# A fixed order for TensorE in the second pass's heads, and a head's output matmuls one step later

## The chip, the cores and the metric

The kernel runs on one core of one Trainium2 chip. The metric is the device time of one execution in microseconds; lower is better. The figure given for a kernel is the median of several runs, and one further execution is recorded by the hardware profiler. Every line of a profile that is shown here comes from that recorded execution.

## The reference

One layer of a decoder trunk, for one sequence of 2048 tokens and a width of 1024, all in fp32. Cut to what matters:

```python
h = rms_norm(x, g_pre) * (1.0 + scale) + shift
pv, pg, hq, hf, hi, hg, mg_pool, mg_hgrn = split(h @ w_in)      # 1024 -> 7168

# branch A: pooling over windows of 2, 4, 8, 16, gated by silu(pg)
branch_a = (multiscale_pool(pv) @ pool_w * pool_scale * silu(pg)) @ w_pool_o

# branch B: 8 heads of 128, gated linear recurrence
f = lb + (1 - lb) * sigmoid(hf);  k = 1 - f;  q = silu(hq);  v = hi
S_t = diag(f_t) S_{t-1} + k_t v_t^T;   o_t = S_t^T q_t
branch_b = (rms_norm(o, hgrn_norm_g) * silu(hg)) @ w_hgrn_o

y = (sigmoid(mg_pool) * branch_a + sigmoid(mg_hgrn) * branch_b) @ w_out
x = x + gate * rms_norm(y, g_post)
```

The recurrence is evaluated in chunks. Within a chunk the output is (decayed scores of q and k) times v, and between chunks a 128 x 128 state per head is decayed and added to.

## The kernel before, in words

**Passes and stages.** The 2048 tokens are worked in two passes of 1024 (`p` = 0, 1), and each pass in two halves of 512 (`t` = 0, 1; `T` = 512). A pass projects V for all heads, then runs eight heads one after the other, then the projection of branch B and the output projection y. In the profiled execution the heads of the first pass run from 124 to 742 us, what follows of that pass (and V of the second) to 978, the heads of the second pass to 1582, and its projections to the end.

**Weight products.** A weight product is 12 matmuls of 128x512: four blocks of the contraction, three matmuls each, since the activations and weights are held as a high and a low part (`three`). `quad` makes a 2 x 2 block product of the weights and activations out of seven such products (a Strassen scheme) in three PSUM banks: `pa` (B11), `pe` (T1), `pa` (T2), `pb` (B21), `pa` (T3), `pe` (B22), `pa` (T4). Between them ScalarE copies a bank to SBUF (`c22`, `c12`, and `pb` from `pa`), and VectorE adds. A head has three quads: `fq` (gates f and q), `m` (the merge gates) and `gp` (the head's output gate, and pooling), in this order; head 7 has `fq`, `gp`, `m`. A name ends in pass, head and half, so `pam1_3` is the bank `pa` of quad `m` in pass 1 (the second), head 3; the listings of the order below drop the pass and keep the head and the half.

**The recurrence beside the products.** `hgrn(p, h, t, cx)` is a generator that holds one head's recurrence for one half. It is advanced to its next `yield` by each call of `tick()`, and `quad` ticks once after most of its products, so the small matmuls of a head lie between the products of that head and of the next. Both halves go side by side. In the order of a head:

- four steps of scores (`psa`, five ticks apart): in each, 16 matmuls for each half that use 32 columns of TensorE's array; VectorE puts them under a mask into `PT`, and prepares the next operands `X`;
- transposes of K (`pk`), the state's increments (`pd`, 4 matmuls for each half), and VectorE's chain of states (`SC`);
- two ticks later the output matmuls (`po`, 8 for each half), ScalarE's squares with their sums (`junk`, `ss`) and a power on GpSimd;
- two ticks later ScalarE's scaled copies (`on`); two ticks later their transposes (`pot`), VectorE's gate product (`sgg<-pot`) and SyncE's store of the gated half.

A head's last steps fall into the `m` and `gp` quads of the head behind it, beside that head's first scores.

**What sets the order.** The source gives the program's order, and the tile framework's scheduler sets the order on each engine when the kernel is built: an instruction may be issued ahead of one that stands before it in the program. `after(ins)` is a context in which every new instruction is ordered behind `ins`:

```python
    def after(ins):
        return tc.issue_after(ins.ins) if ins is not None else nullcontext()
```

It is an edge for the scheduler; on one engine it puts no wait into the program. Before the change it is used around V's products, the adaLN products and a few others, not in the heads. All matmuls of products and of the recurrence go through `mm`, so they carry its line in the profile (L345; the transposes are L810 for `pk` and L846 for `pot`). PSUM has eight banks: four for the products (`pj`), two for `psa` (`ph`) and two shared by `pk`, `pd`, `po` and `pot` (`px`).

Of the kernel before, what the change touches and what calls it, by code (L numbers as in the profile page):

```python
# [18 lines left out]
P = 128  # L19
# [52 lines left out]
def tile_block(ctx: ExitStack, tc: tile.TileContext, x, c, w_ada, b_ada, g_pre, g_post, w_in,  # L72
# [3 lines left out]
    V, A, G, PE, SP = nc.vector, nc.scalar, nc.gpsimd, nc.tensor, nc.sync  # L76
# [16 lines left out]
    def utile(name, dt=F32):  # L93
        return up.tile([P, T], dt, tag="u", name=name)
# [4 lines left out]
    def after(ins):  # L99
        return tc.issue_after(ins.ins) if ins is not None else nullcontext()  # L100
# [23 lines left out]
    ident = cst.tile([P, P], F32, name="ident")  # L124
# [138 lines left out]
    def factor_step(steps):  # L263
        flush_due()
        once(steps)
# [67 lines left out]
    def take(look=LOOK):  # L333
# [7 lines left out]
        ready[i] = None  # L341
        return w if isinstance(w, tuple) else (w[:, 0:T], w[:, T:2 * T])

    def mm(o, l, r, start, stop):
        return PE.matmul(o, lhsT=l, rhs=r, start=start, stop=stop, skip_group_check=True)  # L345

    def three(ps, w, rhs, start, stop):

# [38 lines left out]
    def ada_mul(q):  # L387

        for kk in range(KT):
            o = psa[1][32 * (kk % 4):32 * (kk % 4) + 32, :]  # L390
            it = PE.matmul(o, lhsT=cz[:, kk, :], rhs=parts[q][kk], start=kk < 4, stop=kk >= 4, skip_group_check=True)
        sums[q] = utile(f"ar{q}")
        behind["ar"] = A.copy(sums[q], psa[1])
        return it

    def ada_done(q):
        r = sums.pop(q)
        for j in range(4):
            it = PE.transpose(psa[0][:, j * P:(j + 1) * P], r[:, j * P:(j + 1) * P], ident)
        v = small[:, 56:60]  # L400
        V.tensor_reduce(v, psa[0].rearrange("p (j a b) -> p j a b", j=4, b=32)[:, :, :, 0], axis=AX.X, op=ADD)
        sl = slice(q * 2, q * 2 + 2)
        V.tensor_tensor(shv[:, sl], v[:, 0:2], col("bsh")[:, sl], op=ADD)
        V.tensor_tensor(scv[:, sl], v[:, 2:4], col("bsc")[:, sl], op=ADD)
        iv = V.scalar_tensor_tensor(scv[:, sl], scv[:, sl], 1.0, col("gpre")[:, sl], op0=ADD, op1=MUL)
        return it, iv
# [6 lines left out]
    def pv_load(g):  # L413
        wt = [utile(f"pvt{g}_{z}") for z in range(2)]
        for z in range(2):
            SP.dma_start(wt[z], w_pv_t[g * P:(g + 1) * P, z * T:(z + 1) * T])
        return wt
# [75 lines left out]
    def xsq(tok, xs):  # L493

        s2 = sp.tile([P, 2], F32, tag="xss", name=f"xss{tok}")
        for n in range(2):
            jx = sp.tile([P, T], BF16, tag="jx", name=f"jx{tok}_{n}", bufs=1)
            A.activation(jx, xs[n], AF.Square, scale=1.0 / 32, accum_out=s2[:, n:n + 1])
        r = rst[:, tok:tok + 1]
        G.tensor_scalar(r, s2[:, 0:1], s2[:, 1:2], EPS, op0=ADD, op1=ADD)  # L500
        tt(r, r, mh[:, 0:1], op=ALU.pow, e=G)
        return r

    def x_rows(tok, load):
        xs = [utile(f"x{tok}_{n}") for n in range(2)]
        for n in range(2):
            load(xs[n], x[tok * P:(tok + 1) * P, n * T:(n + 1) * T])
        return xs
# [52 lines left out]
    def x_stats(tok):  # L561
        xsq(tok, x_rows(tok, gated))
# [105 lines left out]
    def hgrn(p, h, t, cx):  # L668
# [6 lines left out]
        K = utile("K" + n)  # L675
# [5 lines left out]
        o = 0  # L681
# [112 lines left out]
        for cc in range(NT):  # L794
            o = cc * P
# [11 lines left out]
        yield  # L807
        pk = px.tile([P, T], F32, tag="px", name="pk" + n)
        for cc in range(NT):
            PE.transpose(pk[:, cc * P:(cc + 1) * P], K[:, cc * P:(cc + 1) * P], ident)  # L810
        KS = utile("KS" + n)
        A.copy(KS, pk)
        yield
# [6 lines left out]
        for cc in range(NT):  # L820
            nxt = SC[:, cc * P:(cc + 1) * P]
            V.scalar_tensor_tensor(nxt, sts[-1], Tb[128][:, cc:cc + 1], pd[:, cc, :], op0=MUL, op1=ADD)
            sts.append(nxt)
        yield
        yield
        po = px.tile([P, NT, P], F32, tag="px", name="po" + n)
# [12 lines left out]
        on = utile("on" + n)  # L839
# [3 lines left out]
        yield  # L843
        pot = px.tile([P, T], F32, tag="px", name="pot" + n)
        for cc in range(NT):
            PE.transpose(pot[:, cc * P:(cc + 1) * P], on[:, cc * P:(cc + 1) * P], ident)  # L846
        og = cx["G"].pop((h, t))
        V.scalar_tensor_tensor(og, pot, col("ng"), og, op0=MUL, op1=MUL)
        two_out("G", p, h, t, og, cx, h == NH - 1)
# [3 lines left out]
    def pv_got(p, g, t, u, cx):  # L853
        n = f"{p}_{g}_{t}"
        w = WINDOWS[g]
        PV = qp.tile([P, HALO + T], F32, tag="qr", name="PV" + n)
        A.copy(PV[:, 0:HALO], halo[:, g, :])
        A.copy(PV[:, HALO:], u)
        A.copy(halo[:, g, :], PV[:, T:T + HALO])
        cur, lo = PV, 0  # L860
        sh = 1
        while sh < w:
            nx = qp.tile([P, HALO + T], F32, tag="qr", name=f"W{sh}_{n}")
            lo += sh
            tt(nx[:, lo:], cur[:, lo:], cur[:, lo - sh:HALO + T - sh], op=ADD)
            cur = nx
            sh *= 2
        pm = utile("pm" + n)
        V.scalar_tensor_tensor(pm, cur[:, HALO:], 1.0 / w, PV[:, HALO:], op0=MUL, op1=SUB)
        if p == 0 and t == 0:  # L870
            e0 = pm[:, 0:HALO]
            tt(e0, cur[:, HALO:2 * HALO], icnt[:, g * HALO:(g + 1) * HALO])
            tt(e0, e0, PV[:, HALO:2 * HALO], op=SUB)
        cx["pw"][g, t] = pm

    def pg_got(p, g, t, u, cx):
        n = f"{p}_{g}_{t}"
        sg = utile("spg" + n)
        A.activation(sg, u, AF.Sigmoid)
        tt(sg, u, sg)  # L880
        V.scalar_tensor_tensor(sg, cx["pw"].pop((g, t)), col("psc", g), sg, op0=MUL, op1=MUL)
        two_out("P", p, g, t, sg, cx, g == NG - 1)

    def g_got(p, h, t, u, cx):
        sg = utile(f"sgg{p}_{h}_{t}")
        A.activation(sg, u, AF.Sigmoid)
        tt(sg, u, sg)
        cx["G"][h, t] = sg
# [42 lines left out]
    def v_head(p, h, cx):  # L931
        vt = vp.tile([P, 8, P], F32, tag="v", name=f"V{p}_{h}")
        gated(vt, cx["Vd"][:, :, h * P:(h + 1) * P], "Vd")
        cx["V"][h] = vt
# [91 lines left out]
    def two_split(nm, i, cx):  # L1026
        for t in range(2):
            hi, lo = cx["g" + nm][i, t]
            split(lo.bitcast(F32), hi, lo)
# [261 lines left out]
    def once(steps):  # L1291

        if steps:
            steps.pop(0)()
# [10 lines left out]
    it = ada_mul(0)  # L1305
    with after(ix), after(ic):
        prep()
    with after(it), after(ix):
        it, iv = ada_done(0)
# [45 lines left out]
    for p in range(NPASS):  # L1355
# [60 lines left out]
        def htick():  # L1416
            tick()
            every[0] += 1
            if every[0] % 11 in (1, 3, 5, 7, 9):
                factor_step(behind_heads)  # L1420

        for h in range(NH):
            if 0 < h < NH - 1:
                v_head(p, h + 1, cx)
            n = f"{p}_{h}"

            def fq(row, t, u):
                (f_got, q_got)[row](p, h, t, u, cx)

            def gp(row, t, u):  # L1430
                if row == 1:
                    g_got(p, h, t, u, cx)
                elif h % 2 == 1:
                    pg_got(p, h // 2, t, u, cx)
                else:
                    pv_got(p, h // 2, t, u, cx)

            wt = pv_load(h // 2) if p == 0 and h % 2 == 0 else None
            steps = []

            def tick_in():
                htick()
                once(steps)

            quad("fq" + n, cx, fq, htick)
            if h == 0:
                for z in range(2):
                    v_head(p, z, cx)
            active.extend(hgrn(p, h, t, cx) for t in range(2))
            if wt:  # L1450
                pv_merge(h // 2, wt)
            htick()
            for i, kind in enumerate(KINDS[h == NH - 1]):
                if kind == "gp":
                    quad("gp" + n, cx, gp, htick)
                else:
                    if h == NH - 1:
                        steps += [lambda: None]
                        steps += [lambda g=g: two_in("P", p, g, cx) for g in range(NG - 1)]
                        steps += [lambda g=g: two_split("P", g, cx) for g in range(NG - 1)]  # L1460
                    quad("m" + n, cx, lambda row, t, u: m_got(p, h, row, t, u, cx), tick_in)
                htick()
            while steps:
                once(steps)
            if p + 1 < NPASS:
                x_stats(8 + h)
        for j in range(KT):
            if j > 0:
                two_in("G", p, j - 1, cx)
            if j > 1:  # L1470
                g_half(p, j - 2, cx)
                if j % 2 == 1:
                    forms("g", j // 2 - 1, cx["g32"])
            a_job(p, j, cx)
            factor_step(behind_heads)
# [101 lines left out]
```

## Time and profile before

| | before |
|---|---|
| median of 3 runs | 1743.84 us (1743.43 to 1744.43) |
| profiled execution | 1744.35 us |
| its span | 1742.6 us |
| mean granted TensorE clock | 0.999 |
| TensorE matmuls, busy | 1714.9 us (98% of the span) |
| TensorE weight loads, busy | 1402.0 us (80%) |
| VectorE busy | 1220.8 us (70%) |
| ScalarE busy | 852.3 us (49%) |
| GpSimd busy | 101.5 us (6%) |
| HBM | 243 GB/s over the span |

The span runs from the first to the last instruction of the recorded execution, and the time of that execution adds what lies around it. An engine's busy time is the time in which it has an instruction under way; matmuls are pipelined, and their ends are modelled, so 98% does not say that TensorE runs at its peak. Matmul records are counted in passes through the array: an fp32 matmul of scores or state shows as two records.

### The profile page before, as it was taken

Reading aid. Unit: us, or ns where it says so; the run is one execution under the profiler, and the core shown is the slowest. Engines: PE = TensorE matmul, PEld = TensorE weight load, DVE = VectorE, ACT = ScalarE, POOL = GpSimd, SP = SyncE. Lnnn points to the kernel's source line nnn. Section 1 sums busy time; section 2 is a strip of 40 time slices with the busy share of each in tenths; the row PEclk is TensorE's granted clock in tenths of the full one; section 3 lists DMA queues with packets and bytes.
Section 4 is the critical chain, followed back from the end, with each engine's and each line's share of the span. In section 5 each row is a group of like instructions: output and inputs, shape, how many; then the busy total and the mean of one; then the engine's idle time right before and its main releaser. Section 6 shows DMA issues by size and latency. Waiting matters only on the chain.

```text
span 1742.6 us, 31732 instructions
## 1 busy us (share of the span) xinstructions
PE 1714.9 (98%) x11805; PEld 1402.0 (80%) x11805; DVE 1220.8 (70%) x2546; ACT 852.3 (49%) x1975; POOL 101.5 (6%) x152
## 2 busy tenths in 40 slices
PE   7999999999999999999999999999999999999998
PEld 4788888888887887877887888888788888888886
DVE  4668898897988889778787255455455545676666
ACT  4756656566565665343755325344243353434243
POOL 1100001000100100100030000000000000000002
PEclk9999999999999999999999999999999999999999
DMA  9759787788779787976895765665665655575657
GB/s 311 269 177 327 282 322 266 292 298 312 267 285 337 261 286 283 341 263 209 277 309 169 250 203 181 202 199 169 218 194 170 215 174 195 176 236 164 215 193 266
DMA packets 191288, 425.33 MB, mean 244 GB/s; under 512 B 19311, under 2 KB 44572, under 8 KB 191134
## 3 DMA queue, kind: packets, MB, share of 16 engines
q1 hardware_dynamic: 181918, 406.52, 68.3%
q10 hardware_dynamic: 9216, 16.78, 2.6%
q8 instruction: 93, 1.52, 0.4%
q14 instruction: 61, 0.50, 0.1%
HBM read 267.51 MB, written 155.71 MB: 243 GB/s over the span
## 4 chain that ended last, share of the span: by engine, by line
PE 88%; DMA 5%; DVE 4%; ACT 1%; issue 1%; SPq 0%; POOL 0%; DVEq 0%; POOLq 0%; ACTq 0%
PE pafq L345 10%; PE pam L345 9%; PE pagp L345 9%; PE pefq L345 5%; PE pem L345 5%; PE pegp L345 5%; PE psA L345 4%; PE ray L345 4%; PE psa L345 3%; PE psV L345 3%; PE raB L345 3%; PE po L345 3%; PE pbfq L345 3%; PE pbm L345 2%; PE pbgp L345 2%; PE raV L345 2%
## 5 line engine op out<-in xcount | busy, mean ns | idle before, releaser
L181 DVE TENSOR_TENSOR whl<-wr,whl 128x512 fp32r<-128x512 f32 x160 | 109.0, 688 | 47.4 <-ACT whl L181 45.8
L345 PE MATMUL pagp<-hT,whl 128*128 128x512 f32 x384 | 128.2, 395 | 1.1 <-DVE c22gp L490 0.8
L345 PE MATMUL pam<-hT,whl 128*128 128x512 f32 x384 | 129.0, 397 | 0.1
L181 ACT CAST whl<-wr 128x512 fp32r<-128x512 f32 x160 | 99.1, 622 | 59.2 <-issue 15.3
L345 PE MATMUL pafq<-hT,whl 128*128 128x512 f32 x384 | 126.3, 390 | 0.0
L724 DVE COPY_PREDICATED PT<-mask,psa 128x256 f32<-128x256 uint8 x160 | 86.0, 546 | 46.4 <-PE psa L345 46.4
L181 ACT CAST whl<-wri 128x512 fp32r<-128x512 f32 x76 | 47.2, 623 | 119.3 <-PE psA L345 28.0
L345 PEld LDWEIGHTS pagp<-hT,whl 128*128 128x128 f32 x384 | 72.1, 188 | 17.2 <-issue 1.2
L345 PEld LDWEIGHTS pam<-hT,whl 128*128 128x128 f32 x384 | 72.2, 188 | 15.0 <-ACT c12m L626 0.3
L345 PEld LDWEIGHTS pafq<-hT,whl 128*128 128x128 f32 x384 | 72.1, 188 | 15.1
L345 PE MATMUL psA<-Ph,whl 128*128 128x512 f32 x256 | 82.3, 395 | 0.6 <-ACT Ph L181 0.4
L345 PE MATMUL psV<-whl,hB 128*128 128x512 f32 x256 | 79.6, 394 | 1.2 <-ACT hB L1315 1.1
L490 DVE TENSOR_TENSOR K<-K,TT 128x256 f32<-128x256 f32 x192 | 80.2, 422 | 0.4 <-PE psa L345 0.4
L345 PE MATMUL pagp<-lT,whl 128*128 128x512 f32 x192 | 74.9, 390 | 0.0
L345 PE MATMUL pam<-lT,whl 128*128 128x512 f32 x192 | 74.9, 390 | 0.0
L345 PE MATMUL pafq<-lT,whl 128*128 128x512 f32 x192 | 74.7, 389 | 0.0
L345 PEld LDWEIGHTS psa<-X,K 128*32 128x32 f32 x2816 | 50.0, 110 | 26.5 <-issue 20.2
L181 DVE TENSOR_TENSOR whl<-wri,whl 128x512 fp32r<-128x512 f32 x76 | 51.6, 683 | 26.0 <-ACT whl L181 25.2
L835 POOL TENSOR_SCALAR ss<-ss 128x4 f32<-128x4 f32 x32 | 14.3, 448 | 878.2 <-ACT junk L834 878.0
L672 DVE TENSOR_SCALAR F<-F 128x512 f32<-128x512 f32 x16 | 6.8, 426 | 78.1 <-ACT F L671 78.0
L345 PE MATMUL psa<-X,K 128*32 128x48 f32 (+2 forms) x2816 | 60.6, 208 | 0.5 <-DVE PT L718 0.5
L345 PEld LDWEIGHTS psV<-whl,hB 128*128 128x128 f32 x256 | 47.5, 188 | 13.9 <-issue 1.7
(569 smaller groups left out, 4810.3 us busy)
## 6 DMA issues: line engine op xcount, KB each, us to landing
wr<-in_w_quad_dram SPq DMA_DIRECT2D x88, 256.0 KB, 5.0
whl<-scr_y SPq DMA_DIRECT2D x36, 512.0 KB, 4.6
sm<-Sd SPq DMA_DIRECT2D x64, 256.0 KB, 5.4
whl<-scr_b SPq DMA_DIRECT2D x32, 512.0 KB, 3.3
scr_y<-rfy SPq DMA_DIRECT2D x40, 256.0 KB, 3.0
x<-in_x_dram SPq DMA_DIRECT2D x32, 256.0 KB, 3.7
wa<-in_w_ada_dram SPq DMA_DIRECT2D x32, 256.0 KB, 6.1
V<-Vd SPq DMA_DIRECT2D x16, 512.0 KB
```

Source lines behind the costliest of these rows:

```text
L181: return A.copy(hi, src32), (e or V).tensor_tensor(lo, src32, hi.bitcast(F32), op=SUB)
L345: return PE.matmul(o, lhsT=l, rhs=r, start=start, stop=stop, skip_group_check=True)
L490: return (e or V).tensor_tensor(o, a, b, op=op)
L672: V.tensor_scalar(F, F, 1e-30, None, op0=MAX)
L724: V.copy_predicated(dst.rearrange("p (c q) a b -> p c q a b", c=NT), m, src.rearrange("p c (a b) -> p c a b", b=b).unsqueeze(2) .broadcast ...
L835: G.tensor_scalar(ss, ss, 1.0 / P, EPS, op0=MUL, op1=ADD)
```

## The change

It has two parts. First, `mm` and a new `turn` (a transpose) put every TensorE instruction of the second pass's heads behind the one that the program issued before it, so there TensorE's order is the program's; `line["on"]` is set ahead of the heads loop when `p > 0` and cleared behind it. Second, `hgrn` has one more `yield` ahead of `po`, in both passes: the output matmuls and all that follows in that head come one tick later.

```diff
+    line = {"on": False, "it": None}
+
     def mm(o, l, r, start, stop):
-        return PE.matmul(o, lhsT=l, rhs=r, start=start, stop=stop, skip_group_check=True)
+        with after(line["it"] if line["on"] else None):
+            line["it"] = PE.matmul(o, lhsT=l, rhs=r, start=start, stop=stop, skip_group_check=True)
+        return line["it"]
+
+    def turn(o, i):
+        with after(line["it"] if line["on"] else None):
+            line["it"] = PE.transpose(o, i, ident)
...
         for cc in range(NT):
-            PE.transpose(pk[:, cc * P:(cc + 1) * P], K[:, cc * P:(cc + 1) * P], ident)
+            turn(pk[:, cc * P:(cc + 1) * P], K[:, cc * P:(cc + 1) * P])
...
             sts.append(nxt)
+        yield
         yield
         yield
         po = px.tile([P, NT, P], F32, tag="px", name="po" + n)
...
         for cc in range(NT):
-            PE.transpose(pot[:, cc * P:(cc + 1) * P], on[:, cc * P:(cc + 1) * P], ident)
+            turn(pot[:, cc * P:(cc + 1) * P], on[:, cc * P:(cc + 1) * P])
...
+        line.update(on=p > 0, it=None)
         for h in range(NH):
...
+        line["on"] = False
         for j in range(KT):
```

Eight lines come in ahead of `three` and one in `hgrn`, so `mm` is L348 after, `turn` L353, `junk` L843 and `on` L850.

**TensorE, second pass, around `pegp` of head 3.** A row is one instruction or a run of alike ones: line, operation, out<-in, tile of the array or of the output, count. `pagp` and `pegp` are products of the quad `gp`, `psa` the scores of head 3 (`psa_0` and `psa_1` are its halves), `pot` the transposes of head 2's output. Before, the first product of `gp` ends and the second stands between the scores:

```order
L345 MATMUL pagp_3_13346<-lB_3_9933,whl_13221 128x512
L345 MATMUL pagp_3_13346<-hB_3_9932,whl_13221 128x512
L345 MATMUL psa_0_10924<-X_1_3_0_13257,K_3_0_13062 32x48 x2
L345 MATMUL pegp_3_13363<-hT_0_10287,whl_13288 128x512
...
L345 MATMUL pegp_3_13363<-hT_3_10378,whl_13288 128x512
L345 MATMUL psa_0_10924<-X_1_3_0_13257,K_3_0_13062 32x48 x14
L345 MATMUL psa_1_10925<-X_1_3_1_13282,K_3_1_13069 32x48 x16
L345 MATMUL pagp_3_13346<-hT_0_10405,whl_13315 128x512
```

After, at the end of `pegp`:

```order
L348 MATMUL pegp_3_13349<-lT_3_10379,whl_13288 128x512
L348 MATMUL pegp_3_13349<-hT_3_10378,whl_13288 128x512
L353 MATMUL pot_2_0_13366<-ident,on_2_0_13322 128x128 x4
L353 MATMUL pot_2_1_13373<-ident,on_2_1_13327 128x128 x4
L348 MATMUL psa_0_10924<-X_1_3_0_13257,K_3_0_13062 32x48 x16
L348 MATMUL psa_1_10925<-X_1_3_1_13282,K_3_1_13069 32x48 x16
L348 MATMUL pagp_3_13332<-hT_0_10405,whl_13305 128x512
```

The scores, in two groups around `pegp` before, are one group behind it, and `pot`, which stood ahead of `pagp`, stands right ahead of them. The same holds around `pefq` in five heads (three scores were ahead of it, none now), for `pd` around `pem` in seven heads (2 and 6 before, 8 behind it now), and `po` moves from behind `pbm` to behind the next `pam` in seven heads. In head 7 scores and transposes that alternated become `pam`, eight `pot`, `pem`, then all scores of the step.

**ScalarE, second pass, head 3, the end of quad `m`.** `on` and `junk` are head 2's scaled copies and squares, `c12m` and `sgm` sigmoids of products of `m`, `Sd` the stores that ScalarE issues. Before:

```order
L834 ACTIVATE junk_1_2_1_13217,ss_2_1_13210<-po_2_1_13200 128x128
L841 ACTIVATE on_2_1_13310<-po_2_1_13200,ss_2_1_13210 128x128 x4
...
L892 ACTIVATE c12m_3_13156<-c12m_3_13156 128x512
L893 DMA Sd_3_0_198<-c12m_3_13156 128x512
L892 ACTIVATE sgm_3_1_13329<-pam_3_13072 128x512
L893 DMA Sd_3_1_199<-sgm_3_1_13329 128x512
L631 COPY pbgp_3_13347<-pagp_3_13346 128x512
```

After:

```order
L901 ACTIVATE sgm_3_1_13319<-pam_3_13072 128x512
L850 ACTIVATE on_2_0_13322<-po_2_0_13196,ss_2_0_13206 128x128
L902 DMA Sd_3_1_199<-sgm_3_1_13319 128x512
L850 ACTIVATE on_2_0_13322<-po_2_0_13196,ss_2_0_13206 128x128 x3
L850 ACTIVATE on_2_1_13327<-po_2_1_13217,ss_2_1_13227 128x128 x4
L639 COPY pbgp_3_13333<-pagp_3_13332 128x512
```

The scaled copies stood ahead of the last two sigmoids of `m`; they now stand behind the sigmoid of `pam`'s last product and ahead of the copy of `pagp`.

**VectorE, first pass, head 5.** `sgg_4` is the gate product of head 4, `X_0_5` the next score operands of head 5, `whl` and `rfy` weights being split and formed. Before:

```order
L490 TENSOR_TENSOR sq_5_1_5676<-sq_5_1_5676,TT_5_1_5873 128x32x8
L848 SCALAR_TENSOR_TENSOR sgg_4_0_5483<-pot_4_0_6106,vec,sgg_4_0_5483 128x512
L181 TENSOR_TENSOR whl_6086<-wr_5968,whl_6086 128x512
L848 SCALAR_TENSOR_TENSOR sgg_4_1_5424<-pot_4_1_6113,vec,sgg_4_1_5424 128x512
L181 TENSOR_TENSOR whl_6125<-wr_5974,whl_6125 128x512
L490 TENSOR_TENSOR X_0_5_1_6212<-sq_5_1_5676,TT_5_1_5873 128x16x16
```

After:

```order
L498 TENSOR_TENSOR sq_5_1_5676<-sq_5_1_5676,TT_5_1_5873 128x32x8
L498 TENSOR_TENSOR ray_5786<-ray_5786,ray_5782 128x512
L498 TENSOR_TENSOR X_0_5_1_6212<-sq_5_1_5676,TT_5_1_5873 128x16x16
L498 TENSOR_TENSOR sq_5_0_5763<-sq_5_0_5763,TT_5_0_5865 128x8x32
L498 TENSOR_TENSOR X_0_5_0_6369<-sq_5_0_5763,TT_5_0_5865 128x256
L857 SCALAR_TENSOR_TENSOR sgg_4_0_5483<-pot_4_0_6150,vec,sgg_4_0_5483 128x512
L181 TENSOR_TENSOR whl_6111<-wr_5932,whl_6111 128x512
L857 SCALAR_TENSOR_TENSOR sgg_4_1_5424<-pot_4_1_6157,vec,sgg_4_1_5424 128x512
```

The gate products moved behind the score operands. The first pass is not tied; its TensorE order moves too, by `po`'s extra tick: the scores of a step now lie between the two `pot` groups in heads 1 to 6.

## The prediction

> **What bounds the kernel now.** I read the page's engine sums, then busy time by stage, then the chain of waits inside one head. The head stage of the second pass runs from 978 to 1582 us; the stages (from, to, then busy time by engine) read:
>
> ```profile
> core 0: us, PE busy (x) PEld busy (x) DVE busy (x) ACT busy (x) POOL busy (x), PEclk, DMA share, GB/s
> 124.00:742.00 618.00, 615.08 (x4835) 505.53 (x4835) 535.11 (x1152) 360.02 (x872) 40.97 (x50) 1.00 0.83 297
> 978.00:1582.00 604.00, 603.89 (x4772) 498.48 (x4771) 333.27 (x805) 242.25 (x631) 19.62 (x32) 1.00 0.60 196
> ```
>
> TensorE is busy for 603.89 of 604.00 us there at full clock; VectorE (55%), ScalarE (40%) and the DMA engines (0.60) have room. So TensorE's own work is the bound, and idle time can give at most 0.11 us. The first row is the same stage of the first pass: VectorE is at 87% and TensorE waits a few times.
>
> Is there anything to gain in a TensorE that never idles? The chain of waits in the second pass's head 2 (start, length, what, matmul records) says yes:
>
> ```profile
> 1156.84 0.87 PE pot L846 x8
> ...
> 1160.45 0.21 PE psa L345 x4
> 1160.66 2.95 PE pegp L345 x12
> 1163.61 0.81 PE psa L345 x60
> 1164.41 2.94 PE pagp L345 x12
> 1167.35 2.72 PE pbgp L345 x12
> ...
> 1178.23 0.82 PE psa L345 x64
> 1179.05 2.94 PE pafq L345 x12
> ```
>
> A weight product of 12 matmuls takes 2.72 us, but 2.94 to 2.95 right behind score matmuls (psa), which use 32 columns of the array. A score group so costs its own piece and 0.22 us of the product behind. (A score matmul shows as two records: x64 is the 32 of one step.) The step split in two costs 0.21 + 0.81 + 2.95 + 2.94 - 2 x 2.72 = 1.47; the same step whole (1178.23) 0.82 + 2.94 - 2.72 = 1.04. A split costs **0.43 us**, all of it counted as busy.
>
> The Trainium skill, "Trainium Kernel Development and Optimization", section Performance Expectations, calls matmul busy time a bad metric of the distance to the limit, since matmuls are pipelined, and prefers the busy share of LDWEIGHTS. By busy time the second pass's term would be 0.1 us; by the page it has no such lid (LDWEIGHTS is at 498.48 of 604), and the chain above agrees with the page.
>
> Small matmuls on all 128 columns do not have this cost. More rows of the chain of head 2:
>
> ```profile
> 1134.05 0.44 PE pd L345 x4
> ...
> 1137.23 1.34 PE pd L345 x12
> ...
> 1144.03 3.57 PE po L345 x32
> 1147.60 2.76 PE pam L345 x12
> ```
>
> The product behind po is 2.76, and 0.44 + 1.34 is 16 times the 0.11 of one record: joining the two pd groups, as the tied order does, and moving po gain 0.04 us a time at most. I put both at nothing.
>
> **The change, part by part.** Second pass, order tied.
>
> (a) Scores around pegp (2 then 14 + 16 of them before, together now), heads 0 to 6: 7 x 0.43 = 3.0 us.
>
> (b) Scores around the first four products of the next head's fq quad (3 then 13 + 16), heads 1, 2, 3, 4 and 6. Head 2 is split, head 5 already whole:
>
> ```profile
> 1111.93 0.24 PE psa L345 x5
> 1112.17 2.95 PE pefq L345 x12
> ...
> 1123.28 1.46 PE psa L345 x44
> 1124.73 2.99 PE pefq L345 x12
> ...
> 1332.99 1.52 PE psa L345 x48
> 1334.51 2.94 PE pefq L345 x12
> ```
>
> (The chain passes over records that end early, so it counts 49 of 64.) Split: 0.24 + 1.46 + 2.95 + 2.99 - 2 x 2.72 = 2.20; whole: 1.52 + 2.94 - 2.72 = 1.74. Five times 0.46 is 2.3 us.
>
> (c) Head 7 has transposes and scores mixed:
>
> ```profile
> 1509.07 0.66 PE pot L846 x4
> 1509.73 0.37 PE psa L345 x18
> 1510.10 0.65 PE pot L846 x4
> 1510.76 2.75 PE pem L345 x12
> 1513.51 0.64 PE psa L345 x46
> 1514.15 2.99 PE pam L345 x12
> ```
>
> That is 8.06 us. Whole it is 0.87 (pot) + 2.72 + 0.82 (psa) + 2.94 = 7.35: 0.7 us.
>
> (d) New neighbours: po right ahead of scores (7 heads), pot right ahead of scores (7 heads). Does a score group cost more there? The first pass has one case, in order of time:
>
> ```profile
> 367.30 0.39 PE L345 MATMUL po<-SC,sq 128*128 128x128 f32 x2
> 367.61 0.36 PE L345 MATMUL psa<-QR,K 128*32 128x48 f32 x10
> ...
> 368.24 0.39 PE L345 MATMUL pam<-lT,whl 128*128 128x512 f32 x1
> ```
>
> The two last po records leave at 0.11 each, so po ends its issue at 367.52; pam's second matmul is at 368.24, one pitch (2.72/12 = 0.23) after where its first would be: 0.49 us for 10 records. By the chain, 4 records cost 0.21 + 0.23 = 0.44 and each more (0.81 - 0.21)/56 = 0.011: 0.50 for 10. No surcharge behind po. Behind pot, row (c) has psa 0.1 to 0.2 dearer, but there pot follows it too. I take 0; bounds 0 and 14 x 0.15 = 2.1 us.
>
> (e) What is released later. po and all behind it move by a product: po now runs after pam's third product, `on` after the fourth, pot after pegp. The waits behind it: ScalarE's squares (junk) wait for po, the `on` copies now stand behind the sigmoid of pam's last product, VectorE's gate product waits for pot, SyncE's store of the gate for that. ScalarE's prices:
>
> ```profile
> 1222.51 1.14 ACT L841 ACTIVATE on<-po,ss 128x128 f32<-128x128 f32 x4 [1.40 <-POOL ss L490]
> ...
> 1226.93 0.60 ACT L892 ACTIVATE sgm<-pam 128x512 f32<-128x512 f32 x1 [0.44 <-PE pam L345]
> 1227.56 0.33 ACTq L893 DMA_DIRECT2D Sd<-sgm  x1
> ```
>
> From the end of pam's fourth product: 0.60 + 0.33 + 2 x 1.14 = 3.2 us; the products of pagp and pegp ahead of pot cover 2 x 2.72 = 5.4. It is hidden with 2.2 us to spare. VectorE's two gate products now land together with the score masks, but VectorE is 45% idle. On SyncE's queue the load of V waits for po:
>
> ```profile
> SPq L116 <- PE po L345: 26.1, 13, 3.2
> ```
>
> It now stands behind one more weight load, and the next weight load needs a buffer that pem frees, 2.7 us after po is done: no cost. Sum of the second pass: 3.0 + 2.3 + 0.7 = **6.0 us less**.
>
> First pass: untied, but po's extra step reorders it. Split score groups: head 1 one more, head 2 one fewer, head 4 one more, head 7 six before and six now: +0.4. In heads 1 to 6 the scores now lie between the two pot groups. The extra in (c) was 8.06 - 0.87 - 2 x 2.72 - (0.37 + 0.22 + 0.64 + 0.22) = 0.3, less the pot latency that the scores hide, so 0.1 to 0.2: +0.9.
>
> The Trainium skill, "TensorEngine Tiling (Array Packing)", section Key Properties, says that a change of tiling mode drains the array. By that rule alone scores between transposes change mode as often as scores between products, the +0.9 would be 0 and the total 0.9 us lower; the row in (c) speaks for a surcharge.
>
> Against that stand the first pass's waits (who, for whom, total us, times, longest): the first two and the last of six, 2.6 us together:
>
> ```profile
> PE pagp L345 <- DVE c22gp L490: 0.8, 1, 0.8
> PE psa L345 <- DVE PT L718: 0.5, 1, 0.5
> ...
> PE psA L345 <- DVE sm L490: 0.2, 1, 0.2
> ```
>
> The first two are VectorE's backlog in head 5:
>
> ```profile
> 521.27 0.69 DVE L181 TENSOR_TENSOR rfy<-rsy,rfy 128x512 fp32r<-128x512 f32 x1 [2.30 <-ACT X L785]
> 523.42 0.74 DVE L848 SCALAR_TENSOR_TENSOR sgg<-pot,vec,sgg 128x512 f32<-128x512 f32 x1
> 538.66 0.68 DVE L490 TENSOR_TENSOR c22gp<-pagp,c22gp 128x512 f32<-128x512 f32 x1
> ```
>
> VectorE lost 2.30 us waiting for a ScalarE copy that stood behind work on po, then took 15.2 us without a pause (31 instructions) to c22gp. Now that copy stands ahead of `on`, and 26 instructions lie between the gate product and c22gp. I expect both waits gone, -1.3. First pass: +0.4 + 0.9 - 1.3 = 0. Its bounds: all 2.6 us of waits gone and no surcharge, -2.2; or waits kept and VectorE's two gate products (1.5 us) late once in each of two heads, +1.3 + 3.0 = +4.3.
>
> **Sum.** 6.0 us less. The profiled execution took 1744.35 us (span 1742.6), 0.5 above the median 1743.84 of three runs; it gives 1738.3, and beside the median **1737.8 us**.
>
> **Rivals.**
> *No change.* Joining groups gives nothing, because the new neighbours cost what the split did: (d) at 14 x 0.43 = 6.0 us; 1744. Row 367.61 speaks against it for po, nothing does for a pot with no pot behind.
> *The first pass takes it back.* There VectorE is at 87%, and a gate product two steps later meets the masks and c22gp. At +2 to +4.3: 1739.8 to 1742.1. For it: pagp already waited 0.8. Against it: fewer VectorE instructions ahead of c22gp.
> *Slower.* One mechanism: ScalarE reaches `on` late in the second pass, and since TensorE's order is tied, pot blocks the scores behind it, where before a scheduler could fill in. It decides from 2.2 (the cover to spare) + 6.0/7 = 3.1 us of lateness behind each of the seven heads. At 4.0 us: 7 x 1.8 - 6.0 = +6.6, 1750.4. Against it: ScalarE is 40% busy.
> *More.* The first pass loses all its waits and has no surcharge (-2.2): 1735.6.
>
> **How the numbers follow.** The forecast 0.66 (own range 1736.4 to 1739.4), more gain 0.08, first pass takes it back 0.13 (half of it within 0.2%), no change 0.09, slower 0.04. What a measurement can tell from no change is 0.2%, 3.5 us: faster is below 1740.4. Faster: 0.66 + 0.08 + 0.06 + 0.02 = 0.82; within: 0.13; slower: 0.05. The range leaves out the two far ends: 1735.4 to 1741.2.
>
> **What would show it.** In the profile after: psa pieces of x64 alone in the second pass's heads; the head stage about 6.0 us shorter with TensorE still without idle time; pot x8 followed by psa with no wait for `on`; no wait of pagp on c22gp in head 5. Wrong would be: a product behind psa over 2.95, a psa piece behind pot longer than 0.82, waits of pot on ScalarE in the second pass, or new waits on VectorE in the first.

## The result, and the profile after

| | before | after |
|---|---|---|
| median of 6 runs | 1744.13 us | 1736.53 us (1735.28 to 1737.92) |
| profiled execution | 1744.35 us | 1735.28 us |
| its span | 1742.6 us | 1733.5 us |
| TensorE matmuls, busy | 1714.9 us | 1708.2 us (99%) |
| TensorE weight loads, busy | 1402.0 us | 1405.6 us |
| VectorE / ScalarE busy | 1220.8 / 852.3 us | 1219.8 / 855.6 us |

The ratio after to before is 0.9954, 95% interval 0.9944 to 0.9963: 7.6 us less. The forecast was 1737.8, the range 1735.4 to 1741.2. The profiled execution of after is 1.25 us below its median, that of before 0.2 above, so their difference, 9.1, is a little too large.

To place the gain, the spans are cut at marks that the order fixes: a pass's heads run from the first matmul of its first `pafq` to the first of the `rxB` that follows. Busy time by engine in the two head stages (from, to, length, then the engines), before and then after:

```profile
124.06:741.63 617.57, 614.65 (x4834) 505.17 (x4833) 534.74 (x1151) 359.78 (x871) 40.97 (x50) 1.00 0.83 298
978.33:1581.78 603.45, 603.34 (x4770) 498.04 (x4768) 333.06 (x804) 242.22 (x630) 19.62 (x32) 1.00 0.60 196
```

```profile
123.98:739.49 615.51, 614.19 (x4833) 506.43 (x4832) 533.74 (x1151) 360.01 (x870) 35.90 (x50) 1.00 0.84 299
975.27:1572.66 597.39, 597.39 (x4769) 499.43 (x4768) 331.37 (x802) 243.78 (x628) 19.43 (x32) 1.00 0.62 198
```

The second pass's heads are 6.06 us shorter (603.45 to 597.39), with TensorE idle for 0.1 us before and not at all after: the same matmuls, and time that the profile counted as busy. The first pass's heads are 2.06 shorter, and there TensorE's idle time fell, from 2.92 to 1.32. The other 0.9 us between the two profiles lies between the head stages (236.70 and 235.78 us); among the runs below that stretch takes 235.6 to 238.9, and none of it is put down to the change.

The chain of waits in the second pass's head 2 after (start, length, what, matmul records), which answers to the chain shown of before:

```profile
1141.93 3.57 PE po L348 x32
1145.51 0.82 PE psa L348 x64
1146.32 2.95 PE pem L348 x12
...
1154.71 2.73 PE pegp L348 x12
1157.44 0.87 PE pot L353 x8
1158.31 0.82 PE psa L348 x64
1159.13 2.97 PE pagp L348 x12
```

Every score step is one piece, with 0.82 us of its own and 2.94 to 2.97 for the product behind, but for the last of head 7, which is split before and after (10 and 54 records). Scores right behind `po` or `pot` cost what they cost between products, to 0.03 us, and `pot` follows `pegp` without a wait for `on`.

In head 7 the profile has `pam`, `pem`, the eight `pot`, then the scores (`pam` starts at 1497.92, `pem` at 1500.64, `pot` at 1503.37): `pot` stands behind `pem`, and not ahead of it as the section on the change has it.

TensorE's waits in the first pass's heads after (who, for whom, total us, times, longest); two of the six before are left, and the last is new:

```profile
PE psA L348 <- ACT Ph L181: 0.4, 1, 0.4
PE pagp L348 <- ACT c12gp L634: 0.4, 1, 0.4
PE pvm L348 <- ACT KS L820: 0.3, 1, 0.3
```

### The profile page after: what moved, and what is told of

It reads as the page before. It is cut to its first block, busy times and chain, and to the rows that moved or that the text cites. A ratio compares the mean times of both kernels' runs of the same rounds, so it can differ in the third digit from the quotient of the medians.

```text
span 1733.5 us, 31740 instructions
## 1 busy us (share of the span) xinstructions
PE 1708.2 (99%) x11805; PEld 1405.6 (81%) x11805; DVE 1219.8 (70%) x2546; ACT 855.6 (49%) x1975; POOL 95.9 (6%) x152
## 4 chain that ended last, share of the span: by engine, by line
PE 93%; DVE 2%; DMA 2%; ACT 2%; issue 1%; SPq 1%; POOL 0%; DVEq 0%; POOLq 0%; ACTq 0%
PE pam L348 10%; PE pagp L348 10%; PE pafq L348 10%; PE pem L348 5%; PE psA L348 5%; PE pefq L348 5%; PE psV L348 5%; PE pegp L348 5%; PE raB L348 4%; PE ray L348 4%; PE psa L348 4%; PE po L348 3%; PE pbfq L348 2%; PE pbm L348 2%; PE pbgp L348 2%; PE raV L348 2%
## 5 line engine op out<-in xcount | busy, mean ns | idle before, releaser
L348 PE MATMUL pagp<-hT,whl 128*128 128x512 f32 x384 | 128.1, 394 | 0.4 <-ACT c12gp L634 0.4
L348 PE MATMUL pam<-hT,whl 128*128 128x512 f32 x384 | 128.2, 394 | 0.2
L348 PE MATMUL pafq<-hT,whl 128*128 128x512 f32 x384 | 126.3, 390 | 0.0
L348 PEld LDWEIGHTS pagp<-hT,whl 128*128 128x128 f32 x384 | 72.1, 188 | 16.2 <-ACT c12gp L634 0.5
L348 PEld LDWEIGHTS pam<-hT,whl 128*128 128x128 f32 x384 | 72.1, 188 | 15.4 <-ACT c12m L634 0.6
L348 PEld LDWEIGHTS pafq<-hT,whl 128*128 128x128 f32 x384 | 72.1, 188 | 15.2 <-ACT c12fq L634 0.2
L348 PE MATMUL psA<-Ph,whl 128*128 128x512 f32 x256 | 82.5, 395 | 0.4 <-ACT Ph L181 0.4
L348 PE MATMUL psV<-whl,hB 128*128 128x512 f32 x256 | 80.8, 400 | 1.6 <-ACT hB L1324 1.1
L348 PE MATMUL pagp<-lT,whl 128*128 128x512 f32 x192 | 74.9, 390 | 0.0
L348 PE MATMUL pam<-lT,whl 128*128 128x512 f32 x192 | 74.8, 390 | 0.0
L348 PE MATMUL pafq<-lT,whl 128*128 128x512 f32 x192 | 74.7, 389 | 0.0
L726 DVE COPY_PREDICATED PT<-mask,psa 128x256 f32<-128x256 uint8 (+1 forms) x96 | 52.1, 543 | 21.7 <-PE psa L348 21.7
L348 PEld LDWEIGHTS psa<-X,K 128*32 128x32 f32 x2816 | 48.5, 110 | 19.4 <-issue 17.1
L857 DVE SCALAR_TENSOR_TENSOR sgg<-pot,vec,sgg 128x512 f32<-128x512 f32 x32 | 23.1, 746 | 56.0 <-PE pot L353 56.0
L348 PEld LDWEIGHTS psV<-whl,hB 128*128 128x128 f32 x256 | 48.2, 191 | 14.6 <-ACT hB L181 1.7
```

Of the source, the lines that this page charges most:

```text
L348: line["it"] = PE.matmul(o, lhsT=l, rhs=r, start=start, stop=stop, skip_group_check=True)
L726: V.copy_predicated(dst.rearrange("p (c a) b -> p c a b", c=NT), m.unsqueeze(1).broadcast_to(shp), src.unsqueeze(2).broadcast_to(shp))
```

## The experiments

All runs in one table; each was timed in five rounds against the kernel before. The last two columns are the lengths of the head stages in that kernel's profile, cut at the same marks.

| kernel | median us | ratio to before (95%) | first pass's heads | second pass's heads |
|---|---|---|---|---|
| before | 1743.6 to 1744.3 | | 617.57 | 603.45 |
| the whole change | 1736.53 | 0.9954 (0.9944 to 0.9963) | 615.51 | 597.39 |
| whole_again | 1735.99 | 0.9957 (0.9945 to 0.9970) | 615.73 | 597.39 |
| tie_only | 1742.57 | 0.9991 (0.9982 to 1.0000) | 618.02 | 602.04 |
| step_only | 1742.31 | 0.9988 (0.9980 to 0.9997) | 615.60 | 603.45 |
| step_p2 | 1737.68 | 0.9965 (0.9953 to 0.9978) | 617.73 | 597.39 |
| step_h6 | 1737.48 | 0.9964 (0.9950 to 0.9977) | 616.79 | 597.31 |
| pot_free | 1739.15 | 0.9974 (0.9964 to 0.9984) | 617.82 | 598.26 |
| halves_apart | 1745.68 | 1.0011 (1.0002 to 1.0020) | 615.95 | 605.58 |
| tie_both_nostep | 1751.80 | 1.0040 (1.0026 to 1.0054) | 626.23 | 601.00 |
| join_p1 | 1736.28 | 0.9960 (0.9947 to 0.9972) | 616.35 | 597.39 |
| join_p1_gp | 1733.72 | 0.9945 (0.9932 to 0.9959) | 613.42 | 597.39 |
| join_p1_h5 | 1733.53 | 0.9945 (0.9933 to 0.9958) | 613.76 | 597.39 |

The second pass's stage repeats to 0.1 us where the order is the same, except in tie_only and tie_both_nostep (602.04 and 601.00), which the last section takes up. Of the first pass, the kernels with its order of before gave 616.79 to 618.02 (five, mean 617.6), those with its order of after 615.51 to 615.95 (four, mean 615.7).

**The whole change once more, beside others.**

> The whole change again, beside the others on the same chip: 1736.5 within 1.5 us, and in its profile the second pass's heads 6.0 us shorter than before.

1735.99, and 597.39 in the second pass's heads, 6.06 less than before.

**The tied order alone.** The edit to the changed kernel:

```diff
             sts.append(nxt)
         yield
         yield
-        yield
         po = px.tile(...)
```

> The tied order of the second pass's heads alone, without the extra step ahead of po. There the score groups of the second pass fall from 46 to 33, as in the whole change; pot stays ahead of pagp and po ahead of pam, and the first pass keeps its order of before. Theory (a split score group costs TensorE 0.43 to 0.46 us, and joining them is the gain): 13 joins x 0.46 = 6.0 us less in the second pass, nothing in the first, about 1738. Rival (the gain needs the later po, since in a tied order TensorE waits for the scaled copies and for VectorE's masks): waits on ScalarE or VectorE in the second pass's heads eat the gain, 1742 to 1744.

1742.57: the rival's time, by a wait as it has it, but at one place. Up to head 7 this kernel gained as the whole change did (heads 0 to 6 of the second pass take 475.1 us, 475.2 in the whole change, 480.4 before); then one wait took most of it back. The chain of waits in its head 7:

```profile
1491.15 2.77 PE pagp L348 x12
...
1493.94 0.69 DVE c22gp L498
...
1498.36 0.52 DVE c12gp L498
...
1500.81 0.67 DVE spg L889
...
1501.51 0.05 ACT Ph L181
...
1502.03 1.14 ACT on L849 x4
...
1503.22 2.14 PE pot L353 x8
1505.36 3.31 PE pam L348 x12
```

and ScalarE's instructions in that time (with the idle time before, and its releaser):

```profile
1498.90 0.63 ACT L887 ACTIVATE spg<-c12gp 128x512 f32<-128x512 f32 x1 [3.22 <-DVE c12gp L498]
...
1501.51 0.62 ACT L181 CAST Ph<-spg 128x512 fp32r<-128x512 f32 x1 [1.67 <-DVE spg L889]
1502.03 2.16 ACT L849 ACTIVATE on<-po,ss 128x128 f32<-128x128 f32 x8
```

In head 7 `gp` comes ahead of `m`, so `pot` of head 6 follows `gp`'s last product. ScalarE's order has the pooling branch's `spg` and `Ph` ahead of `on`, and both wait for VectorE, 3.22 and 1.67 us. `on` starts at 1502.03; TensorE, tied, stands with `pot` and runs nothing else. The page gives 2.8 us of wait there:

```profile
PE pot L353 <- ACT on L849: 2.8, 1, 2.8
```

The loss against the tie with the step is 602.04 - 597.39 = 4.65: the wait, and behind it `pot` takes 2.14 instead of 0.87 and `pam` 3.31 instead of 2.72 (1.86 more; what that is stands in the last section).

**The extra step alone.**

```diff
-        line.update(on=p > 0, it=None)
+        line.update(on=False, it=None)
```

> The extra step ahead of po alone, in both passes, without the tied order. The second pass has 47 score groups there (46 before), the first pass the order that it has in the whole change. Theory: second pass +0.4; first pass what the whole change gave there, 3.0 by the two profiles and perhaps 1.6 by the medians; in all 1.2 to 2.6 less, about 1742. Rival (the later po is the cause of the gain): 5 us less or more, 1739 or below.

1742.31, and the theory held but for one term: first pass 615.60, the whole change's; second pass 603.45, as before, where 0.4 more was expected for the 47th group. That group lies in head 7, which became 0.08 us longer; why not 0.4 was not tested. Alone, the parts are worth 1.7 and 2.0 us, together 7.6. By these medians 3.9 is missing in the sum; by the stage lengths it is the 4.65 that the tie loses without the step.

**The step in the second pass alone, and for one head alone.** The first edit makes the extra step hang on the pass, the second on one head:

```diff
-        yield
+        if p > 0:                        # step_p2
+            yield
...
+        if p > 0 and h == NH - 2:        # step_h6
+            yield
```

> The whole change, but the extra step in the second pass alone, so the first pass keeps its order of before. Theory (second pass 6.0 less, and what is beyond comes from the first pass's order): 1738, 1 to 3 us above the whole change, with the first pass's waits of before on c22gp, PT and on. Rival (the first pass's part is spread between executions, not the order): same as the whole change within 0.5 us.

> Tied order in the second pass's heads, and the extra step ahead of po for head 6 of the second pass alone (its po and pot fall into head 7). Theory (the tied order is worth 6.0, and without the step one wait of pot on the scaled copies in head 7, 2.8 us with 2 us more around it, took 4.7 of that back): that wait is gone, second pass 6.0 less, as with the step in all of its heads: 1738, within 1 us of step_p2. Rival (the step has its worth in every head): about 1742, as with no step.

1737.68 and 1737.48, and 597.39 and 597.31 in the second pass: the step has its whole worth there in head 6, whose `po` and `pot` fall into head 7. In that pass the other heads' steps move work and change no time. Head 7's `on` is no earlier: its copies end about 4 us behind `gp`'s last product in tie_only and in the whole change alike (1501.98 there, with the product's end at 1497.92). But with the step `pam` and `pem`, two products of 2.72, lie between that product and `pot`, which so starts 1.4 us behind the copies. The medians lie 1.0 to 1.7 above the whole change with overlapping intervals; that the rest comes from the first pass is shown by the stage lengths, 615.7 against 617.6. Of the waits that step_p2 was to keep there, those on `PT` (0.5) and on `on` (0.4) were there, and that on `c22gp` was not.

**pot left out of the tie, without the step.**

```diff
-            turn(pot[:, cc * P:(cc + 1) * P], on[:, cc * P:(cc + 1) * P])
+            PE.transpose(pot[:, cc * P:(cc + 1) * P], on[:, cc * P:(cc + 1) * P], ident)
```

> The tied order of the second pass's heads without the extra step, as in tie_only, but with the pot transposes left out of the tie. The scheduler then moves one group alone: head 6's pot from ahead of head 7's pam to behind its first product. Score groups stay 33. Theory (the loss in tie_only is TensorE waiting in its fixed order for that pot): the wait of 2.8 us is covered by the product, second pass about 6.0 less, 1738. Rival (the scaled copies are late wherever pot stands): a wait of pot on ScalarE of 2 us or more stays, 1741 or above.

The scheduler moved one head's `pot` behind one product. The wait fell from 2.8 to 0.4 and the stage to 598.26, 0.87 above the joined order without waits. So in tie_only the loss was TensorE standing in its fixed order for that one group. The median, 1739.15, lies between the two expectations, nearer to the theory.

**The price of a group, by itself.**

```diff
         yield
         yield
+        if p > 0 and t == 1:
+            yield
         scores(QR)
```

> The whole change, but in the second pass the second half of each head starts its score steps one tick later, so that the 16 matmuls of each half stand apart, with a product between, in most steps: 56 score groups in the second pass instead of 33. No work is added. Theory (each group has a fixed price): 23 x 0.43 = 9.9 us more than the whole change, about 1746.5, with TensorE still without idle time in the second pass's heads, and about +10 in that stage alone. Rival (the price goes by matmuls, and joining helped by other means): same as the whole change, 1736.5.

1745.68: 9.2 to 9.7 above the whole change, with no work added. 8.19 lies in the second pass's heads (605.58 - 597.39), where TensorE stays busy throughout; most of the rest in the tail, where the projection of branch B waits 0.9 us for a gate product. The chain of waits in head 2:

```profile
1134.65 0.89 PE pd L348 x8
1135.54 2.73 PE pam L348 x12
1138.27 0.89 PE pd L348 x8
1139.16 2.74 PE pbm L348 x12
...
1149.83 1.78 PE po L348 x16
1151.61 0.48 PE psa L348 x32
1152.09 2.94 PE pam L348 x12
```

`pd`, `po` and `pot` are cut in two as well, and their halves add up to the whole (for `pd` 0.89 + 0.89, for `po` twice 1.78 where the whole took 3.57). Two halves of scores cost 2 x (0.48 + 2.94 - 2.72) = 1.40, one whole step 0.82 + 2.94 - 2.72 = 1.04: 0.36 for an even cut, and 8.19/23 = 0.36. The price is by group, as the theory has it, though less than it had: it is 0.36 for an even cut and 0.43 for the cut of 4 and 60 records of before.

**The first pass tied too, without the step.**

```diff
-        line.update(on=p > 0, it=None)
+        line.update(on=True, it=None)
...
-        yield
```

> The tied order in the heads of both passes, without the extra step. Score groups 33 in each pass (50 and 46 before). Theory: second pass 6.0 less; first pass 17 joins x 0.43 = 7.3 less, with its 2 us of waits kept; about 1730.5. Rival (in the first pass VectorE is busy for 87% and the split groups are how the scheduler covers its lateness; a tied TensorE then waits for masks and score operands): 7 us or more of new waits on VectorE in the first pass, 1738 or above.

Slower, 1751.80. The rival's time came, its mechanism only in part. TensorE's waits in the first pass's heads add up to 14.3 us (2.6 before); the first three of seven:

```profile
PE pot L353 <- ACT on L849: 4.8, 2, 4.6
PE pvm L348 <- ACT KS L820: 4.0, 3, 2.0
PE pafq L348 <- ACT c12fq L634: 1.7, 3, 0.9
```

Not the scores wait for masks; transposes, the pooling weights' small matmuls (`pvm`) and products wait for ScalarE's copies, and a tied TensorE has nothing to put ahead of them. Waits that VectorE ended are 1.7 of the 14.3. The longest is head 7's `pot` again, and there VectorE's work stands behind ScalarE's, as in tie_only (`spg` ahead of `Ph` and `on`). What the joins gave shows in the busy time alone, 611.91 in place of 614.65, less than the 7.3 expected; the granted clock also fell twice in these heads (last section).

**Joins in the first pass without the tie.** Two edges (`line["prod"]` and `line["score"]` are the last product and score matmuls) join a step's scores and leave `pot`, `po`, `pk` and `pd` free:

```diff
+            with after(line["score"] if line["join"] and k == 0 else None):
                 mm(ps, wh, rh, start and k == 0, False)
...
+                with after(line["prod"] if line["join"] and i == 0 else None):
+                    line["score"] = mm(s48[...], K[...], X[:, i, :], True, True)
```

`line["join"]` is set for all heads of the first pass in join_p1, beside the `gp` quads of heads 0 to 6 in join_p1_gp, in heads 0 to 5 in join_p1_h5.

> The whole change, and in the first pass two order edges only: a score step's first matmul stands behind the product issued before it in the program, and the next product's first matmul behind the step's last score; po, pot, pk and pd of the first pass stay free. Score groups of the first pass 38 instead of 51. Theory: 13 x 0.43 = 5.6 us less than the whole change, about 1731. Rival (joined scores wait for VectorE's masks and operands in the first pass, where the tied order of both passes gave 15 us of waits): 5 us or more of new waits, 1736 or above.

> The whole change, and in the first pass the two order edges of join_p1 around the scores beside the gp quads of heads 0 to 6 alone: score groups 42 there instead of 51. Theory (a join is worth 0.34 to 0.40, and the waits of join_p1 stood in the m quads and in head 7): 9 x 0.37 = 3.3 us less in the first pass's heads, the 1.3 us wait of the pooling weights' matmuls on KS perhaps kept; 1733 to 1734.5. Rival (in the first pass each join is given back as a wait on ScalarE or VectorE): within 1 us of the whole change, 1735.5 to 1736.5.

> The whole change, and the two order edges of join_p1 in heads 0 to 5 of the first pass alone: score groups 41 instead of 51. Theory: 10 x 0.37 = 3.7 us less, with the waits of pam on c12m (0.7) and of the pooling weights' matmuls (1.3) kept and those of head 7 gone: about 2 less, 1734. Rival: within 1 us of the whole change, 1735.5 to 1736.5.

join_p1 gained nothing over the whole change: the theory's 1731 did not come, and TensorE waits 5.3 us in those heads, against 1.1. These waits are on ScalarE's copies, where the rival had masks and operands. The first two of five:

```profile
PE pvm L348 <- ACT KS L822: 1.6, 2, 1.3
PE pot L353 <- ACT on L852: 1.2, 1, 1.2
```

The narrower versions keep most of the joins (42 and 41 groups; join_p1 has 38, the whole change 51) and lose most of these waits: head stage 613.42 and 613.76, about 2 us below the whole change, with 1.5 and 2.0 us of waits. They are the fastest here, 1733.72 and 1733.53. Their ratios' intervals overlap with the whole change's, so it is the stage lengths that show this gain.

## Why the prediction was right, point by point

**The bound and (a) to (c).** 6.0 us from joining score groups was forecast, 6.06 measured in the stage, and 33 groups in place of 46 were the cause: the gain was there in every kernel that joined them, in busy time and not in waits, and splitting groups in halves_apart took it away again by the group. It lies in the heads where the sum put it: heads 0 and 5 became 0.42 us shorter (part a alone, 0.43), heads 1 to 4 and 6 by 0.87 to 0.91 (a and b, 0.89), head 7 by 0.80 (c, 0.7). Matmul busy time showed no room, 603.34 of 603.45 us. Weight loads did leave room (498.04 us of the stage before, 499.43 after), but not where it was; the length of the same product behind different neighbours told that.

**(d), new neighbours: 0, right.** `psa` is 0.82 behind `po` and `pot`; the product behind scores behind `pot` takes 2.97 instead of 2.94. That is over the 2.95 that was named as a sign of being wrong, but 0.03 in seven heads is 0.2 us in all. The rival *no change* falls with that.

**(e), what is released later: right for the kernel as changed, but the part was misread.** The prediction looked at `on` as a risk of the extra step. It is the other way round: the step protects the tied order. Without it `pot` waits 2.8 us for head 7's `on`. That is the mechanism of the rival *slower*, at one place; the cover of 5.4 us was worked out for heads whose `gp` follows `m`, and head 7 was not worked out by itself. The sum took no price for it and needed none, since both parts came together; as far as the working goes, that was luck.

**The first pass: the terms that were mis-sized.** Forecast 0 (+0.4 for split groups, +0.9 for scores between transposes, -1.3 for waits), measured -1.9 by the means of the table. VectorE's backlog in head 5 shrank as said: `c22gp` now starts 13.4 us behind head 4's gate product, where it was 15.2.

```profile
523.46 0.75 DVE L857 SCALAR_TENSOR_TENSOR sgg<-pot,vec,sgg 128x512 f32<-128x512 f32 x1
...
536.83 0.69 DVE L498 TENSOR_TENSOR c22gp<-pagp,c22gp 128x512 f32<-128x512 f32 x1
```

The waits fell by 1.5 in all (2.6 to 1.1), not quite by the parts forecast. `psa` waits 0.5 us for `PT` in all five kernels with the first pass's order of before and in none of the four with that of after. But the wait of 0.8 on `c22gp` was mostly that one execution's: the other four with the order of before show 0.2 or none.

The +0.4 and the +0.9 were wrong. TensorE's busy time in these heads was to grow by 1.3 and fell by 0.46 (614.65 to 614.19). Heads 1 and 4, with one score group more, became 0.27 and 0.17 longer, head 2, with one fewer, 0.52 shorter: -0.1 in all. Heads 3, 5 and 6, where only the place and the size of the cuts changed, became 0.02, 0.22 and 0.13 shorter. Chain of waits around `pagp` and `pegp` of head 2 in the first pass, before and after:

```profile
307.24 0.87 PE pot L846 x8
308.11 2.73 PE pagp L345 x12
310.85 0.21 PE psa L345 x4
311.06 2.95 PE pegp L345 x12
314.01 0.80 PE psa L345 x60
314.81 2.94 PE pagp L345 x12
```

```profile
307.22 2.73 PE pagp L348 x12
309.95 0.44 PE pot L353 x4
310.39 0.31 PE psa L348 x16
310.69 0.59 PE pot L353 x4
311.28 2.77 PE pegp L348 x12
314.05 0.65 PE psa L348 x48
314.70 2.99 PE pagp L348 x12
```

10.50 and 10.48 us: scores between transposes cost the same here as scores between products. (The cut is more even after, 16 and 48 records, and the price of a cut that the product behind bore before now falls in part on the second `pot`, 0.59.) That is what the Trainium skill's rule in "TensorEngine Tiling (Array Packing)", section Key Properties, would have given (a drain at each change of tiling mode, wherever it lies). The surcharge of 0.3 had been read off one place in head 7, from a sum of short pieces. Without the +0.9 the forecast would have been 1736.9; the measured time lies between the forecast and the rival *more* (1735.6), nearer to the rival. The first pass's stage differs by 1.2 us from one execution to the next among kernels of the same order, so its mean gain is known less well than the second pass's.

## What to carry to other kernels

An engine that is busy all the time can still be made faster: look for the instruction that takes longer behind a certain neighbour (2.94 against 2.72), count how often that neighbour occurs, and ask whether the order can gather such pieces. A fixed order on the bounding engine is worth its gain only where nothing in it waits: work each place out by itself, the odd head above all, and move the late consumer one step back, or free it alone. Where the other engines are tight, tie only the pieces that belong together.

## What the runs showed of the hardware

A wait can cost more than its length, through TensorE's clock. Where the granted clock falls between the first heads and the end of the second pass's heads, it is 0.50 for 3.41 us and 1.00 around that. In tie_only it fell once there, right behind the 2.83 us wait of `pot` (from, to, length, busy time by engine, then the clock):

```profile
1503.05:1506.45 3.40, 3.23 (x12) 2.63 (x13) 2.01 (x3) 1.63 (x6) 0.00 (x0) 0.50 0.14 53
```

In tie_both_nostep it fell three times, behind waits of 2.00 us (`pvm`), 4.61 us (`pot`) and 1.89 us (`raB`, in the projection of branch B). The fourth row is what follows the 2.83 us wait of `pot` in the second pass's head 7 of that kernel:

```profile
566.90:570.30 3.40, 3.40 (x17) 3.40 (x17) 1.86 (x4) 2.36 (x5) 0.00 (x0) 0.50 1.02 369
672.72:676.12 3.40, 3.16 (x12) 2.40 (x11) 3.40 (x9) 1.83 (x6) 0.00 (x0) 0.50 0.97 314
795.60:799.00 3.40, 3.40 (x9) 2.65 (x8) 1.19 (x2) 1.75 (x3) 0.00 (x0) 0.50 0.85 335
1513.60:1517.00 3.40, 3.00 (x17) 2.42 (x18) 2.10 (x3) 1.49 (x5) 0.00 (x0) 1.00 0.21 78
```

That wait is as long as tie_only's, in the same order of TensorE, and there the clock stayed at 1.00. The stage took 601.00 us in place of 602.04, and the whole difference lies in head 7: the fall cost 1.04 of the 4.65 us, and the wait with `pot` following `on`'s copies one by one (8 in 2.16 us) the other 3.61.

Behind the wait of 1.8 us in the kernel before (V's copies, `rxV1T`) the clock stayed at 1.00, and in all these kernels it did so behind every shorter wait from the first head to TensorE's last product:

```profile
923.70:926.00 2.30, 2.22 (x10) 1.83 (x11) 2.30 (x5) 2.30 (x6) 0.00 (x0) 1.00 0.57 172
```

The Trainium skill, "TensorE: Matmul & The Clock Gate", Part 1, has the clock halved after at least one idle window of about 3.4 us. The half clock agrees; three of the four waits that it followed here, 1.89, 2.00 and 2.83 us, were shorter than that. The length of the wait alone does not decide it, since one of two waits of 2.83 us was followed by a fall and the other was not; what does was not tested.
